# A hybrid decoder layer on one core: another way to the first half of x^T, squares moved to VectorE, a set of sums made a step later, the first gates' operands made earlier, and another last row

## The chip, the core and the metric

The kernel runs on one core of a Trainium2 chip. A core has TensorE (PE; its weight loads are listed as PEld), VectorE (DVE), ScalarE (ACT), GpSimd (POOL) and SyncE (SP), which here only issues DMAs. Each engine works through its own instructions strictly in the order in which they stand, and waits at an instruction until what it needs has been made. The metric is the time of one execution in microseconds (us), smaller is better. Times within a profile are counted from the first instruction.

## The reference

All is float32: 2048 positions of width 1024, one input projection to 6144 columns, two mixers, one output projection.

```python
xn = rms_norm(h, ln_g)
proj = jnp.einsum('bsd,de->bse', xn, w_in)
b_gate, c_gate, x_conv, g_conv, x_lru, g_lru = jnp.split(proj, splits, axis=-1)
y_conv = short_conv_mixer(b_gate, c_gate, x_conv, conv_w)
y_conv = headwise_rms_norm(y_conv, N_CONV_HEADS, conv_out_g) * jax.nn.silu(g_conv)
y_lru = rg_lru_mixer(x_lru, lru_conv_w, lru_conv_b, w_a, b_a, w_i, b_i, lam)
y_lru = headwise_rms_norm(y_lru, N_LRU_HEADS, lru_out_g) * jax.nn.silu(g_lru)
h = h + jnp.einsum('bse,ed->bsd', jnp.concatenate([y_conv, y_lru], axis=-1), w_out)
return rms_norm(h, final_g)
```

`rms_norm` divides each row of x by the root of its mean square. In `rg_lru_mixer` a width-4 convolution u goes through two block-diagonal maps (the gates), a is exp(8 r log_sigmoid(lam)), and a recurrence runs over the positions.

## The kernel before

**Products.** A float32 value is split into a high part (a cast by ScalarE to a type that TensorE multiplies at full rate) and a low part (value minus high part, a subtraction on VectorE or GpSimd, function `low`). A product is three matmuls: high by high, high by low, low by high (`mm`, L959). A 2x2 block product is done in the seven-product way: sums of blocks of the weights (tiles `s`) and of x^T (tiles `th`, `tl`, named T[0..6]; T[6] is the sixth sum, kept as `t6` until it is split). A group of matmuls is 4 pieces j of the contraction times 3.

**Steps.** A step is one set of output columns: `l` (the recurrence's input and gate path), `a` and `b` (the convolution mixer), `o` (output projection). The first three steps are plain: eight blocks each without sums. Step 0 works with c11, c21 on positions 0 to 511 and c12, c22 on positions 512 to 1023; steps 1 and 2 run 8 groups each in `plain`, and while they run the sums of x^T blocks are made (`bit`, functions done two per group by `after1`, then `after2`). From step 3 on a step has seven products, with an A bank whose content is copied out (`q1`, `u2`, `rr`) before the next product adds to it.

**The start.** Rows 0 to 511 of x (`x0[0..3]`) are loaded, squared on ScalarE (`norm_rows`), scaled by 1/root on VectorE, and turned into x^T by 128x128 transposes on TensorE (`turn`: four per 128x512 piece, 16 pieces for 1024 rows); a copy out of PSUM applies ln_g. Rows 512 to 1023 follow in the same way (`second`). The constant klam for the recurrence is made by small VectorE instructions at the very start (`make_klam`, L118 to L138).

**What sets the order.** The whole order is written by hand: the code is run once, and each engine gets its instructions as the code names them. `at(n, f)` puts f off by n calls of `tick()`; there is one tick per group of matmuls. So the recurrence of step 0 (`lru`, called with late=3) has its convolution c0, cj at ticks 1 to 3, `sth` (a cast of u on ScalarE) at 5+3, `stl` (two subtractions 64x1024 on VectorE, tiles `st`) at 6+3, the first gates at 8+3, their sigmoids at 9+3, the second gates at 10+3 (gates have two PSUM buffers, freed by the sigmoids), then products, Tanh, Exp, Sqrt, the scan `s5` and `finish`. `finish` scales a tile `gl` or `gb` (L633) and stores it by DMA to `yd`; these tiles have two buffers, so the step after next fills the buffer (put 22 and 21) only when that store has landed.

**The last row.** In the last step `put` combines each bank, adds the residual `xr`, squares on ScalarE, takes the root, scales by final_g on VectorE and stores; the two blocks of 128 positions go one after the other.

Of the kernel before, what the change touches and what calls it, by code (L numbers as in the profile page):

```python
# [38 lines left out]
def hymba_kernel(ctx: ExitStack, tc: tile.TileContext, x, xt, w_in, par, lamc, w_gate, w_out, final_g, out):  # L39
# [75 lines left out]
    def make_klam():  # L115
# [6 lines left out]
        nc.vector.tensor_scalar(out=acc, in0=s, scalar1=2.0, scalar2=None, op0=ALU.add)
# [390 lines left out]
    def norm_rows(b):
        junk = sp.tile([P, D], F32, tag="s", name="junk")
        ss = small.tile([P, 1], F32, tag="ss", bufs=4, name="ss")
        rs = small.tile([P, 1], F32, tag="rs", bufs=4, name="rs")
        nc.scalar.activation(out=junk, in_=x0[b], func=AF.Square, accum_out=ss)
        nc.scalar.activation(out=rs, in_=ss, func=AF.Sqrt, scale=1.0 / D, bias=eps)

        def scale():  # L520
            nc.vector.reciprocal(out=rs, in_=rs)
            nc.vector.tensor_scalar(out=x0[b], in0=x0[b], scalar1=rs, scalar2=0.0,
                                    op0=ALU.mult, op1=ALU.add)

        return scale

    def turn(c, kt, dst, act):
        pool, tag = ((pss, "s"), (psu, "u"))[act]
        tp = pool.tile([P, C], F32, tag=tag, name="tp")
        for b in range(NB):  # L530
            nc.tensor.transpose(tp[:, b * P:(b + 1) * P], x0[c * NB + b][:, kt * P:(kt + 1) * P], ident)
        g = pt[:, LN_G + kt:LN_G + kt + 1]
        if act:
            nc.scalar.activation(out=dst, in_=tp, func=AF.Copy, scale=g)
        else:
            nc.vector.tensor_scalar(out=dst, in0=tp, scalar1=g, scalar2=None, op0=ALU.mult)
# [793 lines left out]
```

## Time and profile before

| what | us |
|---|---|
| time, median of 3 runs (lowest to highest) | 1340.99 (1340.28 to 1343.42) |
| the profiled execution | 1336.38 |
| its span, first to last instruction | 1334.6 |
| TensorE busy, share of the span | 1293.2, 97% |
| VectorE busy | 1033.8, 77% |
| ScalarE busy | 747.1, 56% |
| GpSimd busy | 230.9, 17% |
| mean granted TensorE clock | 0.993 |

A busy TensorE is not one at its peak: matmuls overlap, so what counts is the distance between their starts and the places where it stands still. A row of the timeline is: start, duration, engine, line, operation, tiles out<-in, shape, count; in brackets the idle time just before and what ended it. A row of the view by windows gives the window, its length, then busy time and count of each engine, the granted clock, the share of the DMA engines and GB/s.

### The profile page before, as it was taken

The numbers are of one execution on the slowest core, as the hardware profiler recorded it, in microseconds if no ns is written. First come the engines' busy times: TensorE is split into PE (matmuls) and PEld (weight loads), VectorE is DVE, ScalarE is ACT, GpSimd is POOL, SyncE is SP. The second block draws the span as 40 slices with busy tenths as digits, with TensorE's granted clock in tenths as the row PEclk, the third lists the DMA queues.
The fourth block names the chain that finished last, engine by engine and source line by source line (L and its number), as shares of the span: only waits on it lengthen the run. The fifth ranks groups of instructions, "written<-read, shape, count | busy, mean of one in ns | idle before, by whom it ended". The sixth has DMA issues, their size and how long they took to land.

```text
span 1334.6 us, 16554 instructions
## 1 busy us (share of the span) xinstructions
PE 1293.2 (97%) x5648; PEld 1056.4 (79%) x5648; DVE 1033.8 (77%) x1245; ACT 747.1 (56%) x1139; POOL 230.9 (17%) x160
## 2 busy tenths in 40 slices
PE   6989999999999999899999999999999999999997
PEld 5867778787878787778888888888888888887886
DVE  7778888899989897978566675667549867648986
ACT  7476757575665757465544545354457433444543
POOL 2204343343344350202010101102010000000000
PEclk9989999999999999999999999999999999999999
DMA  7137897988889889453689999999779888797754
GB/s 290 32 111 254 288 255 281 286 317 295 327 282 336 291 284 327 149 162 111 215 308 304 335 347 332 349 340 365 244 269 324 260 224 238 278 384 258 250 178 165
DMA packets 158804, 355.27 MB, mean 266 GB/s; under 512 B 17920, under 2 KB 52736, under 8 KB 158720
## 3 DMA queue, kind: packets, MB, share of 16 engines
q1 hardware_dynamic: 158432, 353.90, 78.4%
q8 instruction: 45, 0.74, 0.2%
q14 instruction: 39, 0.32, 0.1%
q10 hardware_dynamic: 288, 0.32, 0.1%
HBM read 217.11 MB, written 137.04 MB: 265 GB/s over the span
## 4 chain that ended last, share of the span: by engine, by line
PE 50%; DVE 17%; DMA 12%; issue 8%; ACT 4%; SPq 1%; POOL 1%; DVEq 0%; ACTq 0%; POOLq 0%
PE bank L959 49%; DVE s L163 4%; DVE tl L163 2%; DMA raw<-in_w_in_dram 2%; DMA sd<-s 2%; DMA xr<-od 2%; PE gate L718 2%; DVE u L692 1%; DVE st L163 1%; DMA s<-so 1%; DVE raw L163 1%; DMA tl<-td 1%; DVE sums L623 1%; DVE gl L633 1%; ACT i L725 1%
## 5 line engine op out<-in xcount | busy, mean ns | idle before, releaser
L959 PE MATMUL bank<-th,s 128*128 128x512 f32 x3632 | 1134.2, 391 | 11.4 <-ACT q L1264 4.4
L959 PEld LDWEIGHTS bank<-th,s 128*128 128x128 f32 x3632 | 684.3, 188 | 161.9 <-ACT q L1264 5.7
L959 PE MATMUL bank<-tl,s 128*128 128x512 f32 x1816 | 709.5, 391 | 1.1 <-DVE tl L163 0.9
L959 PEld LDWEIGHTS bank<-tl,s 128*128 128x128 f32 x1816 | 341.9, 188 | 73.8 <-DVE tl L163 2.5
L163 POOL TENSOR_TENSOR s<-raw,s 128x512 fp32r<-128x512 f32 x62 | 111.4, 1809 | 254.1 <-ACT s L200 213.0
L200 ACT CAST s<-raw 128x512 fp32r<-128x512 f32 x140 | 85.0, 617 | 85.2 <-PE bank L959 39.2
L163 POOL TENSOR_TENSOR gb<-gb,sg 128x1024 f32<-128x1024 f32 x16 | 43.4, 2712 | 329.8 <-ACT sg L651 292.1
L163 DVE TENSOR_TENSOR s<-raw,s 128x512 fp32r<-128x512 f32 (+1 forms) x125 | 89.8, 741 | 8.3 <-ACT s L1017 4.4
L163 DVE TENSOR_TENSOR s<-s,s 128x512 fp32r<-128x512 f32 x105 | 85.6, 815 | 3.7 <-ACT s L200 3.7
L163 DVE TENSOR_TENSOR tl<-traw,th 128x512 fp32r<-128x512 f32 x85 | 62.8, 771 | 27.3 <-ACT th L438 13.4
L200 ACT CAST s<-s 128x512 fp32r<-128x512 f32 x105 | 64.6, 615 | 17.0 <-DVE s L163 15.9
L692 DVE SCALAR_TENSOR_TENSOR u<-xl,pt,u 128x1024 f32<-128x1024 f32 x48 | 64.4, 1341 | 6.3 <-ACT u L688 5.8
L1264 ACT COPY q<-bank 128x512 f32<-128x512 f32 x58 | 33.9, 584 | 54.5 <-PE bank L959 45.0
L802 DVE SCALAR_TENSOR_TENSOR t<-p,pt,t 128x1024 f32<-128x1024 f32 x32 | 46.5, 1454 | 14.7 <-ACT t L799 13.9
L725 ACT ACTIVATE r<-gate,pt 64x512 f32<-64x512 f32 x64 | 43.7, 683 | 18.7 <-PE gate L718 17.9
L163 DVE TENSOR_TENSOR st<-u,st 64x1024 fp32r<-64x1024 f32 x32 | 49.5, 1547 | 1.0
L1267 ACT COPY rr<-bank 128x512 f32<-128x512 f32 x31 | 18.1, 583 | 50.4 <-PE bank L959 50.4
L163 POOL TENSOR_TENSOR gl<-gl,sg 128x1024 f32<-128x1024 f32 x16 | 40.3, 2521 | 23.7 <-ACT sg L651 23.7
L725 ACT ACTIVATE i<-gate,pt 64x512 f32<-64x512 f32 x64 | 43.8, 684 | 1.1
L1267 ACT COPY u<-bank 128x512 f32<-128x512 f32 x27 | 15.8, 584 | 50.8 <-PE bank L959 50.7
L163 DVE TENSOR_TENSOR traw<-traw 128x512 f32<-128x512 f32 x60 | 41.8, 699 | 2.6 <-DMA traw<-in_w_out_dram 1.3
L163 DVE TENSOR_TENSOR raw<-raw,zr 128x512 f32<-128x512 f32 x64 | 41.1, 682 | 3.1 <-issue 1.8
(158 smaller groups left out, 1230.9 us busy)
## 6 DMA issues: line engine op xcount, KB each, us to landing
sd<-s SPq DMA_DIRECT2D x151, 512.0 KB
s<-sd SPq DMA_DIRECT2D x151, 512.0 KB
raw<-in_w_in_dram SPq DMA_DIRECT2D x104, 256.0 KB
raw<-yd SPq DMA_DIRECT2D x64, 256.0 KB
traw<-in_w_out_dram SPq DMA_DIRECT2D x64, 256.0 KB
so<-so SPq DMA_DIRECT2D x22, 512.0 KB
s<-so SPq DMA_DIRECT2D x22, 512.0 KB
yd<-gl SPq DMA_DIRECT2D x32, 256.0 KB
```

The lines of the kernel that those rows point to most:

```text
L163: (eng or nc.vector).tensor_tensor(out=out, in0=a, in1=b, op=op)
L200: nc.scalar.copy(dst[i][0], val(i))
L623: nc.vector.tensor_reduce(out=sums[0][:, kt * R:(kt + 1) * R].rearrange("p (q b) -> p q b", q=4), in_=y.rearrange("p (b q a) -> p q b a", ...
L633: nc.vector.scalar_tensor_tensor(out=sil, in0=y, scalar=gain, in1=sil, op0=ALU.mult, op1=ALU.mult)
L692: nc.vector.scalar_tensor_tensor(out=v["u"], in0=o1[:, 1 + j:1 + j + N2], scalar=lw[j], in1=v["u"], op0=ALU.mult, op1=ALU.add)
L718: nc.tensor.matmul(ps[j], v["gw"][n][:, j, :], v["st"][j][:, sl], start=(n == 0), stop=(n == 1))
L725: nc.scalar.activation(out=g_[hi, sl], in_=v["ps"][j][src], func=AF.Sigmoid, bias=pt[src, bias + k:bias + k + 1])
L802: nc.vector.scalar_tensor_tensor(out=tcur["t"], in0=p[:, 2 + j:2 + j + N2], scalar=cw[j], in1=tcur["t"], op0=ALU.mult, op1=ALU.add)
L959: nc.tensor.matmul(bank, a[:, js], b, start=start and n == 0, stop=stop and n == 2, skip_group_check=more)
L1264: nc.scalar.copy(q1, bk["A"])
L1267: nc.scalar.copy(u2, bk["A"])
```

## The change

It has these parts:

1. **x^T of the first half is loaded.** Positions 0 to 511 of x^T come from the transposed copy of x by DMA, two pieces (j and j+4) to a load, 128 x 2 x 512; so do pieces 0 to 3 of positions 512 to 1023. The rows of x are still loaded, for the squares. The roots of the four row blocks (`rs0`) are spread over the partitions by four transposes of a broadcast column into one PSUM bank (`spread`), and each piece is scaled in place by ln_g and that bank (`scaled_t`, one VectorE instruction). Pieces 4 to 7 of positions 512 to 1023 are still turned on TensorE (`turn`, 16 transposes), from rows of which only the right half is scaled.
2. **Two squares on VectorE**: rows 1 and 3 of the first half, by a multiply with a running sum; rows 0 and 2 stay on ScalarE, and one root serves all four. Rows 4, 5 and (6, 7) are squared and scaled one loop pass later than before.
3. **Fifty transposes** of the identity stand first on TensorE (`spin`).
4. **The rest of klam** (22 small VectorE instructions) is made after step 0.
5. **Sums.** `bit` casts first and subtracts one place later; t6 goes to other tiles; the split of the sixth sums moves from step 2 to step 3 (`sixth`).
6. **First gates.** `sth` and `stl` of step 0 come 3 ticks earlier (early=3).
7. **The last row** has a `put_last` of its own, in halves of 512 columns.

```diff
+    def square(b):
+        ss = ss0[b // NB][:, b % NB:b % NB + 1]
+        if b in (1, 3):
+            nc.vector.scalar_tensor_tensor(out=x0[b], in0=x0[b], scalar=1.0, in1=x0[b],
+                                           op0=ALU.mult, op1=ALU.mult, accum_out=ss)
+        else:
+            out = x0[b] if b < NB else sp.tile([P, D], F32, tag="s", name="junk")
+            nc.scalar.activation(out=out, in_=x0[b], func=AF.Square, accum_out=ss)
...
+    def spread(c):
+        rsb[c] = pss.tile([P, C], F32, tag="s", name="rsb")
         for b in range(NB):
+            nc.tensor.transpose(rsb[c][:, b * P:(b + 1) * P],
+                                rs0[c][:, b:b + 1].broadcast_to((P, P)), ident)
+
+    def scaled_t(c, kt, dst):
+        nc.vector.scalar_tensor_tensor(out=dst, in0=dst, scalar=pt[:, LN_G + kt:LN_G + kt + 1], in1=rsb[c],
+                                       op0=ALU.mult, op1=ALU.mult)
...
-                for slots, *fs in ((5, sth), (6, stl), (8, lambda: gates(0)), (9 - h, lambda: sigs(0)),
+                for slots, *fs in ((5 - early, sth), (6 - early, stl), (8, lambda: gates(0)), (9 - h, lambda: sigs(0)),
...
+        def put_last(which, bank, other):
+            i, d = which // 10 - 1, which % 10 - 1
+            tt(ob[i][:, half[d]], bank, other if which == 22 else xr[i][:, half[d]], ALU.add)
+            if which == 22:
+                tt(ob[1][:, half[1]], ob[1][:, half[1]], xr[1][:, half[1]], ALU.add)
+                square(1, 1, 0)
+                tt(xr[1][:, half[0]], xr[1][:, half[0]], sm_u2[0], ALU.add)
+                tt(xr[0][:, half[0]], xr[0][:, half[0]], sm_q1[0], ALU.add)
+            elif which == 11:
+                square(0, 0, 0)
+                bias(1)
+                tt(ob[1][:, half[1]], ob[1][:, half[1]], fg[0][:, half[1]], ALU.mult)
+            elif which == 12:
+                square(0, 1, 2)
+                bias(0)
+                root(0)
+                scaled(0, 0)
+            else:
+                square(1, 0, 2)
+                scaled(0, 1)
+                root(1)
+                scaled(1, 0)
+                nc.scalar.activation(out=ob[1][:, half[1]], in_=ob[1][:, half[1]], func=AF.Copy,
+                                     scale=sq[1][:, 3:4])
+                store(1, 1, nc.scalar)
...
+        spin(50)
+        klam_ = make_klam()
...
+        get_w[0]()
+        get_xt(0)
+        for f in get_w[1:]:
+            f()
+        get_row(4)
+        get_xt(1)
+        get_row(5)
+        get_xt(2)
+        get_row(6)
+        get_xt(3)
+        get_row(7)
...
+            if j:
+                rows(*((4,), (5,), (6, 7))[j - 1])
...
-                put = lru(0, 0, 3)
+                put = lru(0, 0, 3, 3)
...
+        klam_()
         second_half()
...
+        sixths = {1: (2, 1), 3: (0,), 4: (3,)}
...
+                if n == PLAIN:
+                    sixth(*sixths.get(s, ()))
```

Three places show how the order moves. The first is VectorE in steps 1 and 2 before: the last sums of x^T (`traw`, `t6`), a low part of step 2's weights (`s`), the product of the convolution mixer (`p`), the two subtractions `st` for the first gates, then the mixer's convolution (`t`).

```order
L163 TENSOR_TENSOR traw_543<-traw_543,traw_273 128x512
L163 TENSOR_TENSOR tl_787<-traw_543,th_786 128x512
L163 TENSOR_TENSOR t6_790<-traw_273,traw_543 128x512
L163 TENSOR_TENSOR s_792<-raw_598,s_792 128x512
L163 TENSOR_TENSOR p_617<-p_617,xx_807 128x512
L163 TENSOR_TENSOR st_781<-u_619,st_781 64x1024
L163 TENSOR_TENSOR st_782<-u_619,st_782 64x1024
L802 SCALAR_TENSOR_TENSOR t_822<-p_617,pt_164,t_822 128x1024 x2
```

The same engine with the change, from the place where the `st` pair now stands.

```order
L166 TENSOR_TENSOR s_670<-raw_558,s_670 128x512
L166 TENSOR_TENSOR traw_257<-traw_263,traw_257 128x512
L166 TENSOR_TENSOR traw_263<-traw_264,traw_263 128x512
L166 TENSOR_TENSOR st_696<-u_600,st_696 64x1024
L166 TENSOR_TENSOR st_697<-u_600,st_697 64x1024
L166 TENSOR_TENSOR traw_264<-traw_264,traw_257 128x512
L166 TENSOR_TENSOR tl_704<-traw_257,th_703 128x512
L166 TENSOR_TENSOR traw_257<-traw_257,traw_264 128x512
```

The `st` pair is now 14 instructions of 128x512 ahead of the convolution `t`, where it was right ahead of it; the product `p` that `t` needs comes last.

The second is VectorE around the scan of step 0's recurrence (in step 3), before: `u` is the drive, `r` the scan's tile, `s1`, `s2` and `s` belong to step 4's weights, the last row is the scaling of `gl` whose store frees a buffer.

```order
L743 SCALAR_TENSOR_TENSOR u_619<-r_857,u_619 128x1024
L163 TENSOR_TENSOR u_619<-T_957,u_619 128x1024
L163 TENSOR_TENSOR s1_1049<-raw_1012,raw_1014 128x512
L163 TENSOR_TENSOR s2_1051<-s1_1049,raw_1011 128x512
L752 SCALAR_TENSOR_TENSOR r_857<-r_857,u_619 128x1024
L755 COPY hl_187<-r_857 128x1
L163 TENSOR_TENSOR s_1055<-raw_813,s_1055 128x512
L163 TENSOR_TENSOR s_1025<-s2_841,s_1025 128x512
L163 TENSOR_TENSOR raw_1012<-raw_1011,raw_1012 128x512
L633 SCALAR_TENSOR_TENSOR gl_568<-r_857,pt_164,gl_568 128x1024
```

With the change:

```order
L759 SCALAR_TENSOR_TENSOR u_600<-r_836,u_600 128x1024
L166 TENSOR_TENSOR u_600<-T_928,u_600 128x1024
L166 TENSOR_TENSOR tl_1013<-traw_257,th_1012 128x512
L166 TENSOR_TENSOR tl_1017<-rr_677,th_1016 128x512
L166 TENSOR_TENSOR s1_1020<-raw_975,raw_977 128x512
L166 TENSOR_TENSOR s2_1022<-s1_1020,raw_974 128x512
L768 SCALAR_TENSOR_TENSOR r_836<-r_836,u_600 128x1024
L771 COPY hl_187<-r_836 128x1
L166 TENSOR_TENSOR s_1026<-raw_794,s_1026 128x512
L166 TENSOR_TENSOR s_988<-s2_820,s_988 128x512
L166 TENSOR_TENSOR raw_975<-raw_974,raw_975 128x512
L649 SCALAR_TENSOR_TENSOR gl_527<-r_836,pt_164,gl_527 128x1024
```

Two low parts of sixth sums (`tl`) now stand ahead of the scan; their casts (`th`) stand on ScalarE behind the table load and the sigmoid of `gb`.

The third is VectorE at the end of the program, before, from the product of block 0's first half (`ob` is the output tile, `xr` the residual, `fg` final_g).

```order
L163 TENSOR_TENSOR ob_11054<-bank_11157,q1_11076 128x512
L163 TENSOR_TENSOR ob_11054<-ob_11054,xr_11078 128x1024
L163 TENSOR_TENSOR ob_11055<-bank_11121,xr_11057 128x512
L902 RECIPROCAL rs_11186<-rs_11186 128x1
L903 SCALAR_TENSOR_TENSOR ob_11054<-ob_11054,rs_11186,fg_9905 128x1024
L163 TENSOR_TENSOR rs_11204<-ss_11203 128x1
L511 RECIPROCAL rs_11204<-rs_11204 128x1
L920 SCALAR_TENSOR_TENSOR ob_11055<-ob_11055,rs_11204,fg_9905 128x512 x2
```

With the change:

```order
L166 TENSOR_TENSOR ob_11033<-bank_11044,xr_11059 128x512
L946 TENSOR_SCALAR sq_11035<-sq_11035 128x1
L952 RECIPROCAL sq_11035<-sq_11035 128x1
L959 SCALAR_TENSOR_TENSOR ob_11033<-ob_11033,sq_11035,fg_9884 128x512
L166 TENSOR_TENSOR ob_11034<-bank_11102,xr_11038 128x512
L959 SCALAR_TENSOR_TENSOR ob_11033<-ob_11033,sq_11035,fg_9884 128x512
L952 RECIPROCAL sq_11036<-sq_11036 128x1
L959 SCALAR_TENSOR_TENSOR ob_11034<-ob_11034,sq_11036,fg_9884 128x512
```

Behind the last bank (`bank_11102`) there are now two scalings of 128x512 on VectorE, where there were one of 128x1024 and two of 128x512; the other half is scaled on ScalarE.

More of the change, by code (lines that the diff above doesn't have):

```diff
@@ L527, in turn @@
-    def turn(c, kt, dst, act):
-        pool, tag = ((pss, "s"), (psu, "u"))[act]
-        tp = pool.tile([P, C], F32, tag=tag, name="tp")
-        for b in range(NB):
[L531 to L536, printed above, removed]
+    rs0 = [small.tile([P, NB], F32, tag="rs4", bufs=2, name="rs0") for _ in range(2)]
@@ new lines, in hymba_kernel, with spin, turn @@
+    spun = [None]
+    def spin(n):
+        if spun[0] is None:
+            spun[0] = psn.tile([P, 2 * KT * R], F32, tag="sums", name="spin")
+        for _ in range(n):
+            nc.tensor.transpose(spun[0][:, 0:P], ident, ident)
+    def turn(kt, dst):
+        tp = psu.tile([P, C], F32, tag="u", name="tp")
+        for b in range(NB):
+            nc.tensor.transpose(tp[:, b * P:(b + 1) * P], x0[NB + b][:, kt * P:(kt + 1) * P], ident)
+        nc.scalar.activation(out=dst, in_=tp, func=AF.Copy, scale=pt[:, LN_G + kt:LN_G + kt + 1])
@@ L949, in put, with square, bias @@
                 fin(1)
-        return put
+        half = [slice(d * C, (d + 1) * C) for d in range(2)]
+        sq = [small.tile([P, 4], F32, tag="sq", bufs=2, name="sq") for _ in range(2)] if last else None
+        def square(i, d, n):
+            nc.scalar.activation(out=xr[i][:, half[d]], in_=ob[i][:, half[d]], func=AF.Square,
+                                 accum_out=sq[i][:, n:n + 1])
+        def bias(i):
+            nc.vector.tensor_scalar(out=sq[i][:, 1:2], in0=sq[i][:, 0:1], scalar1=1.0 / D, scalar2=EPS,
+                                    op0=ALU.mult, op1=ALU.add)
@@ new lines, in root, with store, scaled @@
+        def root(i):
+            rs = sq[i][:, 3:4]
+            nc.scalar.activation(out=rs, in_=sq[i][:, 2:3], func=AF.Sqrt, scale=1.0 / D, bias=sq[i][:, 1:2])
+            nc.vector.reciprocal(out=rs, in_=rs)
+        def store(i, d, eng):
+            tb = 2 * m + i
+            eng.dma_start(out[tb * P:(tb + 1) * P, half[d]], ob[i][:, half[d]])
+        def scaled(i, d):
+            nc.vector.scalar_tensor_tensor(out=ob[i][:, half[d]], in0=ob[i][:, half[d]], scalar=sq[i][:, 3:4],
+                                           in1=fg[0][:, half[d]], op0=ALU.mult, op1=ALU.mult)
+            store(i, d, nc.sync)
@@ L1170, in after2, with sixth @@
                 low(tr[j][1], T[3, j])
+        def sixth(*js):
+            for j in js:
                 T[6, j] = t_tile(6, j)
```

156 lines of the change are left out of this document (67 added, 89 removed).

## The prediction

> **What bounds the kernel.** I read the page, then TensorE's waits, the windows round the places found, and the timeline there. The first two rows below are of the page and of TensorE's waits, the rest windows.
>
> ```profile
> PE 1293.2 (97%) x5648; PEld 1056.4 (79%) x5648; DVE 1033.8 (77%) x1245; ACT 747.1 (56%) x1139; POOL 230.9 (17%) x160
> ...
> PE gate L718 <- ACT hp L807: 5.5, 1, 5.5
> ...
> PE gate L718 <- DVE st L163: 4.1, 7, 1.3
> ...
> 44.70:72.00 27.30, 27.30 (x121) 22.31 (x119) 23.10 (x30) 13.48 (x22) 4.31 (x4) 1.00 0.05 18
> 72.00:77.50 5.50, 0.03 (x1) 0.00 (x0) 4.07 (x7) 3.85 (x7) 0.00 (x0) 0.69 0.00 0
> 77.50:101.80 24.30, 22.94 (x92) 18.09 (x92) 19.08 (x25) 20.37 (x30) 0.10 (x1) 0.93 0.50 174
> ...
> 600.00:1000.00 400.00, 400.00 (x1762) 330.40 (x1761) 259.17 (x290) 206.36 (x279) 44.85 (x28) 1.00 0.85 293
> ```
>
> TensorE is the bound nearly throughout: from 600 to 1000 it starts a matmul every 400/1762 = 0.227 us, so a group of 12 takes 2.72. The largest single hole is 72 to 77.5, where the first gates wait and the clock drops (0.69; behind it 0.93 over 24.3 us, worth 1.7). Seven waits of gates for `st` say that VectorE is late in later steps too. The timeline of the hole and of the end of the program:
>
> ```profile
> 75.47 0.68 DVE L163 TENSOR_TENSOR p<-p,xx 128x512 f32<-128x512 f32 x1
> 76.19 2.47 DVE L163 TENSOR_TENSOR st<-u,st 64x1024 fp32r<-64x1024 f32 x2
> 76.25 1.15 ACT L799 ACTIVATE t<-p,pt 128x1024 f32<-128x1024 f32 x1 [1.62 <-DVE p L163]
> ...
> 77.55 0.77 PE L718 MATMUL gate<-st,bh 128*128 128x512 f32 x1 [5.53 <-ACT hp L807]
> ...
> 80.88 0.68 ACT L725 ACTIVATE i<-gate,pt 64x512 f32<-64x512 f32 x1
> ...
> 86.75 0.40 PE L959 MATMUL bank<-th,s 128*128 128x512 f32 x1
> ...
> 1326.49 0.39 PE L959 MATMUL bank<-th,s 128*128 128x512 f32 x1
> ...
> 1327.78 1.29 DVE L903 SCALAR_TENSOR_TENSOR ob<-ob,rs,fg 128x1024 f32<-128x1024 f32 x1
> ...
> 1331.15 0.35 ACTq L922 DMA_DIRECT2D out_dram<-ob  x1
> ```
>
> TensorE stood for the `st` pair, which VectorE began only at 76.19; behind the last matmul the last store is issued 4.4 us later.
>
> **Step 0: nothing.** The rows of its terms, in order of time:
>
> ```profile
> 1.21 0.29 POOL masks.py:199 TENSOR_SCALAR_AFFINE_SELECT ident<-ident 128x128 f32<-128x128 f32 x1
> 5.14 1.06 ACT L517 ACTIVATE junk<-x 128x1024 f32<-128x1024 f32 x1 [0.45 <-DMA x<-in_x_dram]
> ...
> 4.00:6.00 2.00, 0.00 (x0) 0.00 (x0) 1.66 (x11) 1.54 (x3) 0.00 (x0) 1.00 1.04 420
> ...
> 11.76 3.04 PE L531 MATMUL tp<-ident,x 128*128 128x128 f32 x13 [0.89 <-DVE x L522]
> 14.45 0.78 PE L959 MATMUL bank<-th,s 128*128 128x512 f32 x1
> 18.42 1.03 PE L531 MATMUL tp<-ident,x 128*128 128x128 f32 x8
> ...
> 30.18 0.61 ACT L1068 CAST th<-traw 128x512 fp32r<-128x512 f32 x1
> 31.43 0.75 DVE L536 TENSOR_SCALAR traw<-tp,pt 128x512 f32<-128x512 f32 x1
> ...
> 33.43 1.30 POOL L163 TENSOR_TENSOR tl<-traw,th 128x512 fp32r<-128x512 f32 x1 [0.76 <-ACT th L248]
> 33.90 1.37 DVE L163 TENSOR_TENSOR s<-raw,s 128x512 fp32r<-128x512 f32 x1 [0.35 <-ACT s L1017]
> ...
> 44.86 0.59 ACT L781 COPY gl<-bank 128x512 f32<-128x512 f32 x1 [2.15 <-PE bank L959]
> ```
>
> The first row block lands at 5.1; at 420 GB/s 0.52 MB takes 1.25, so the fourth lands at 8.9, the first x^T load at 10.8, the next three at 15.2, 17.7, 20.2 and the last row block at 21.5. The fourth square, now on VectorE, ends near 10.2 (1.3, as L903 of the same shape; 0.75 to 1.5 are the ends), root, reciprocal and four transposes give the spread roots at 11.6, scaling (0.75, as L536) and cast bring the first matmul to 13.0 against 14.45. Forty transposes fewer (64 before; 16 and 8 now) are 40 x 0.13 = 5.2 us less on TensorE. But TensorE is not what is late here. Per piece j the chain is two scalings, two casts, a subtraction on VectorE, one of 1.3 on GpSimd; and a VectorE subtraction that meets GpSimd's waits (33.90: 1.37 where it takes 0.69 alone). Going through this engine by engine, the groups of j = 0 to 3 end at 17.9, 21.9, 24.6 and 28.1. ScalarE's order then has the squares of rows 6 and 7 at 26.2 and 27.4 (1.06 and their sums), root at 28.6, scaling of row 7 until 29.95, transposes, copy 0.7, two casts, GpSimd until 33.8, so the first half-group of c12 and c22 ends at 33.8 + 8 x 0.227 = 35.7, and three more with two sets of four transposes at 35.7 + 8.2 + 1.0 = 44.9. Before, `gl` is copied when c22 ends, 44.86. I take no change; ends: 1.5 earlier (the two waits for GpSimd don't happen) and 1.9 later (the third rival). The x^T loads' speed isn't shown at this place; at half speed the last row would land at 26.5, still ahead of its square, so the price is nothing until then.
>
> **Steps 1 and 2: a lead of 2.** Rows:
>
> ```profile
> 3.21 0.17 DVE L122 TENSOR_SCALAR kl<-kl 128x8 f32<-128x8 f32 x1 [0.27 <-ACT kl L120]
> ...
> 7.26 0.16 DVE L138 TENSOR_SCALAR klam<-kl 128x8 f32<-128x8 f32 x1
> ...
> DVE tl L163 <- ACT th L1104: 3.6, 5, 1.4
> ...
> 46.49 0.69 DVE L163 TENSOR_TENSOR s<-raw,s 128x512 fp32r<-128x512 f32 x1 [3.34 <-ACT s L1017]
> ...
> ACT r L725 <- PE gate L718: 1.3, 2, 1.0
> ...
> ACT gb L781 <- PE bank L959: 0.8, 1, 0.8
> ...
> 101.24 0.58 ACT L1264 COPY q<-bank 128x512 f32<-128x512 f32 x1
> ```
>
> The `st` pair goes ahead of 14 instructions and ends near 69.7, so the gates start when TensorE gets there, at 72: 5.5 us and the slow clock behind them are gone. But VectorE's list gets longer: the rest of klam, 7.42 - 3.21 = 4.2 us, now stands behind `s` at 46.5, where nothing hides it, and the 3.6 us of waits for casts go (cast and subtraction stand further apart, VectorE is later). From 46.49 to the end of `st` at 78.66 VectorE took 32.2; now 46.6 + 32.2 + 4.2 - 3.6, less 0.7 for one wait for GpSimd that is shorter, gives `p`, now last, at 78.7 against 76.15. So ScalarE's `t` starts 2.5 later. The sigmoids stand behind it: they end at 80.88 + 0.68 + 2.5 less 0.3 of wait = 83.8, and the second gates need the buffers that these free. TensorE stands there instead, about 80 to 83.8, and the next group starts near 84.2, not 86.75. ScalarE from `t` to the copy `q`: 25.0 before; the waits for TensorE (1.3 + 0.8) and four casts of sixth sums (4 x 0.6) go: 78.75 + 25.0 - 2.1 - 2.4 = 99.3 against 101.24. Lead: 1.9.
>
> **Step 3: most of it given back.** Rows:
>
> ```profile
> 101.83 1.28 ACT L651 ACT_TABLE_LOAD   x1
> ...
> 103.33 2.28 DVE L752 TENSOR_TENSOR_SCAN r<-r,u 128x1024 f32<-128x1024 f32 x1
> ...
> 106.66 2.84 POOL L163 TENSOR_TENSOR gb<-gb,sg 128x1024 f32<-128x1024 f32 x1
> 107.18 2.88 DVE L163 TENSOR_TENSOR s<-s,s 128x512 fp32r<-128x512 f32 x1
> ...
> 110.58 1.27 DVE L633 SCALAR_TENSOR_TENSOR gl<-r,pt,gl 128x1024 f32<-128x1024 f32 x1
> ...
> 115.37 0.69 DVE L163 TENSOR_TENSOR gl<-bank,u 128x512 f32<-128x512 f32 x1 [2.91 <-DMA yd<-gl]
> ```
>
> Two sixth subtractions now stand ahead of the scan, and their casts behind `q`, the table load and the sigmoid: 99.3 + 0.5 + 1.3 + 1.1 + 0.6 = 102.8. With both (1.3) and the two sums (1.3) the scan starts at 105.4, 2.1 later than before. Then `gb` on GpSimd (105.3 to 108.1) lies beside the scan and costs less than at 107.18, where one subtraction waited 2.2 for it; three subtractions, the first ending 0.6 behind GpSimd, and `gl` is scaled at 109.9 against 110.58. The store and the fill of the next `gl` follow at a fixed distance (115.37), and behind that fill stand `xl`, `u` and the copy `q` that TensorE needs in step 4. So **0.7 us** are left. From there on the order is the same, and VectorE is still what gates wait for, so a lead of TensorE alone is lost and 0.7 stays. Ends: -1.5 and the full 1.9 + 1.5.
>
> **The last row: 1.1 us.** The last bank is combined at 1327.4 (VectorE has just scaled a half), squared on ScalarE until 1328.85 with its sum, root 1329.16, reciprocal 1329.4, scaled until 1330.1 on VectorE and ScalarE side by side; last issue 1330.15 against 1331.15, and 256 KB less queued ahead of it. At L903's 1.29 a half is 0.7; the ScalarE half is as L781's copy, 0.6. Ends 0.7 and 1.5.
>
> **Sum.** 0 + 0.7 + 1.1 = 1.8. The profiled execution took 1336.38, so 1334.6; the runs' median is 4.6 above that execution, so I forecast 1340.99 - 1.8 = **1339.2**.
>
> **Rivals.** (1) *The lead is kept.* If ScalarE gets to the sigmoids earlier, or the scan isn't held, TensorE keeps 1.9 + 1.5 and up to the whole hole, 5.5 and 1.7 of slow clock: with the last row's 1.1 that is 4.5 to 8.3, **1332.7 to 1336.5**. For it: gates wait for `st` by 4.1 in all, so VectorE is near enough; against: klam's 4.2 have no cover. (2) *The st pair isn't what the gates lacked* (the change doesn't do what it says): the hole stays, 1340. Against: the pair's start at 76.19. (3) *The spin stays slow.* Ready at 1.5, 50 transposes take 50 x 0.13 = 6.4 at the pace of 18.42, 50 x 0.21 = 10.7 at that of 11.76 (12 intervals of 0.21): they end at 12.2, behind the roots, and all of step 0 is 1.9 later: **1341.1**. The Trainium skill, "TensorE: Matmul & The Clock Gate", section "Part 4: PE-mode transpose", says that transposes don't raise the clock; by that rule the spin would do this. Against it: by 18.42 transposes ran fast, 6.7 us after the slow ones began, and nearly half of that time was transposes. I give it 0.08. (4) *Slower:* the new order still makes VectorE wait 3.6 for casts in steps 1 and 2 (two `st` casts now stand ahead of them on ScalarE). Then `p` is at 82.3, all of step 3 is 3.6 later, from the point where those waits exceed 0.7: 1339.2 + 3.6 = **1342.8**; together with (3) 1344.7.
>
> **Chances.** A measurement tells about 0.3% from no change, 4 us. Forecast 0.48, (1) 0.34, (2) 0.02, (3) 0.08, (4) 0.08. Of these (1) is faster by over 4 us but for a tenth, which the forecast's upper end makes up; (3) and (4) are slower than before, by over 4 only together or with more delay in step 0, about a third of their 0.16: faster 0.34, same 0.61, slower 0.05. The range takes in most of (1), and (4): 1333.0 to 1343.0.
>
> **What would show it.** Right: gates of step 0 start near 72, TensorE stands before the second gates near 80 to 84, the scan later than 103.3, `gl` scaled near 110. Wrong: a matmul stream without a hole from 72 to 100, step 0's c22 copied well before 44 or after 46, or `gl<-bank` before 113.

## The result and the profile after

The changed kernel takes 1348.51 us (median of 6 runs, 1346.93 to 1350.18), the kernel before 1342.55 on the same chip (6 runs, 1340.28 to 1343.42): ratio 1.0051, interval 1.0040 to 1.0062. It is **slower by 6 us**; the forecast was 1.8 faster. On another chip (first experiment) it is 3.9 slower. The profiled execution took 1350.07, span 1347.9. That is 13.7 more than the profiled execution of before, over twice what the medians differ by: the latter (1336.38) is 3.9 below the fastest of the six runs of before. So the two traces are compared here place by place and not by their ends.

The windows of the changed kernel at the same times as those of before, in the last row the third of them before, and some of TensorE's waits (us in all, how often, the longest):

```profile
72.00:77.50 5.50, 5.50 (x24) 4.24 (x23) 5.44 (x9) 1.59 (x3) 0.00 (x0) 1.00 0.00 0
77.50:101.80 24.30, 21.34 (x80) 15.94 (x79) 19.00 (x27) 19.13 (x29) 0.10 (x1) 0.86 0.40 133
101.80:126.00 24.20, 18.64 (x74) 14.60 (x73) 17.07 (x18) 14.80 (x23) 5.54 (x3) 0.93 0.52 193
...
101.80:126.00 24.20, 23.89 (x104) 19.45 (x105) 21.19 (x21) 14.24 (x23) 9.40 (x5) 1.00 0.72 256
```

```profile
PE bank L997 <- ACT q L1340: 6.5, 3, 2.9
PE bank L997 <- ACT u L1346: 5.0, 2, 4.2
...
PE bank L997 <- ACT th L251: 3.3, 1, 3.3
...
PE bank L997 <- DVE s L166: 2.0, 1, 2.0
```

The hole at 72 is gone, as forecast: 24 matmuls in 5.5 us where there was one. But the next two windows start 80 and 74 matmuls instead of 92 and 104. A wait of 3.3 for `th` (the start), one of 4.2 for the copy `u` (step 3) and one of 2.0 for `s` (step 2) are new; the waits for the copies `q` were 4.4 in all before.

The timeline of the start, by engine:

```profile
10.66 0.18 DVE L526 RECIPROCAL rs<-rs 128x4 f32<-128x4 f32 x1 [0.43 <-ACT rs L525]
10.89 0.65 PE L533 MATMUL rsb<-ident,rs 128*128 128x128 f32 x4 [2.11 <-DVE rs L526]
...
12.96 1.41 DVE L537 SCALAR_TENSOR_TENSOR traw<-traw,pt,rsb 128x512 f32<-128x512 f32 x2 [2.12 <-DMA raw<-in_w_in_dram]
...
14.86 0.79 PE L997 MATMUL bank<-th,s 128*128 128x512 f32 x1 [3.32 <-ACT th L251]
...
48.17 0.59 ACT L797 COPY gl<-bank 128x512 f32<-128x512 f32 x1 [2.09 <-PE bank L997]
```

The roots are ready at 10.8 and spread at 11.5, a little ahead of the forecast's 11.6. VectorE waits from 10.8, 2.1 us, until the first x^T load is there too, scales at 12.96 instead of 11.6, and c22 is copied at 48.17 instead of 44.9. (The row names the piece of `w_in` that is in flight with that load; in other executions the same wait is put down to `in_xt_dram`, below.)

The timeline of steps 1 to 3:

```profile
69.21 4.33 DVE L166 TENSOR_TENSOR st<-u,st 64x1024 fp32r<-64x1024 f32 x2 [0.27 <-ACT st L719]
...
81.66 0.69 DVE L166 TENSOR_TENSOR p<-p,xx 128x512 f32<-128x512 f32 x1
...
86.67 0.68 ACT L741 ACTIVATE i<-gate,pt 64x512 f32<-64x512 f32 x1
...
103.70 0.58 ACT L1340 COPY q<-bank 128x512 f32<-128x512 f32 x1
...
104.30 1.28 ACT L667 ACT_TABLE_LOAD   x1
...
105.59 1.06 ACT L667 ACTIVATE sg<-gb 128x1024 f32<-128x1024 f32 x1
...
106.56 0.60 ACT L1244 CAST th<-traw 128x512 fp32r<-128x512 f32 x1
...
107.19 0.69 DVE L166 TENSOR_TENSOR tl<-traw,th 128x512 fp32r<-128x512 f32 x1 [2.64 <-ACT th L1244]
...
109.13 1.67 DVE L166 TENSOR_TENSOR s<-s,raw 128x512 f32<-128x512 f32 x1
...
110.21 2.85 POOL L166 TENSOR_TENSOR gb<-gb,sg 128x1024 f32<-128x1024 f32 x1
...
110.72 4.49 DVE L768 TENSOR_TENSOR_SCAN r<-r,u 128x1024 f32<-128x1024 f32 x1
...
117.14 1.28 DVE L649 SCALAR_TENSOR_TENSOR gl<-r,pt,gl 128x1024 f32<-128x1024 f32 x1
...
118.33 0.69 DVE L166 TENSOR_TENSOR tl<-u,th 128x512 fp32r<-128x512 f32 x1
...
119.11 0.59 ACT L1346 COPY u<-bank 128x512 f32<-128x512 f32 x1 [1.19 <-DVE tl L166]
...
119.75 0.50 PE L997 MATMUL bank<-th,s 128*128 128x512 f32 x1 [4.24 <-ACT u L1346]
...
123.12 0.69 DVE L166 TENSOR_TENSOR gl<-bank,u 128x512 f32<-128x512 f32 x1 [2.89 <-DMA yd<-gl]
```

Read from the copy `q` on: before, the scan started 2.1 behind `q` (103.33 - 101.24) and took 2.28; now it starts 7.0 behind and takes 4.49. VectorE waits 2.64 for the cast of a sixth, which stands on ScalarE behind the table load and the sigmoid `sg`. So the scan comes to lie beside GpSimd's `gb`, where before a subtraction lay (107.18, 2.88 us). Then ScalarE's copy into `u` waits until VectorE, past the scan and `gl`, has read the old `u` for a sixth sum (118.33), and TensorE waits for that copy. `gl<-bank` is 7.75 later than before (115.37).

The end of the program:

```profile
1340.44 0.39 PE L997 MATMUL bank<-th,s 128*128 128x512 f32 x1
...
1343.94 0.38 ACTq L956 DMA_DIRECT2D out_dram<-ob  x1
```

From the last matmul to the last store's issue it is 3.50 instead of 4.66.

### The profile page after: what moved, and what is told of

It is laid out like the page before. It is cut to its first block, busy times and chain, and to the rows that moved or that the text cites. A ratio compares the mean times of both kernels' runs of the same rounds, so it can differ in the third digit from the quotient of the medians.

```text
span 1347.9 us, 16573 instructions
## 1 busy us (share of the span) xinstructions
PE 1304.1 (97%) x5658; PEld 1062.4 (79%) x5658; DVE 1036.4 (77%) x1248; ACT 743.0 (55%) x1129; POOL 229.1 (17%) x160
## 4 chain that ended last, share of the span: by engine, by line
PE 45%; DMA 4%; DVE 3%; issue 1%; ACT 0%; SPq 0%; DVEq 0%
PE bank L997 44%; DMA xr<-od 2%; DMA s<-so 1%; PE gate L734 1%; DVE s L166 1%; DMA tl<-td 1%; DVE raw L166 1%; DVE ob L166 0%; DMA yd<-gl 0%; DMA traw<-in_w_out_dram 0%; DVE tl L166 0%; DMA yd<-gb 0%; DVE ob L919 0%; DVE st L166 0%; DVE sums L639 0%
## 5 line engine op out<-in xcount | busy, mean ns | idle before, releaser
L166 DVE TENSOR_TENSOR s<-s,s 128x512 fp32r<-128x512 f32 x105 | 82.1, 782 | 6.7 <-ACT s L203 6.7
L818 DVE SCALAR_TENSOR_TENSOR t<-p,pt,t 128x1024 f32<-128x1024 f32 x32 | 46.6, 1455 | 16.0 <-ACT t L815 15.2
L166 DVE TENSOR_TENSOR traw<-traw 128x512 f32<-128x512 f32 x62 | 45.8, 741 | 3.1 <-DMA traw<-in_w_out_dram 1.8
L166 DVE TENSOR_TENSOR raw<-raw 128x512 f32<-128x512 f32 x41 | 44.6, 1087 | 0.2
```

Of the source, the lines that this page charges most:

```text
L166: (eng or nc.vector).tensor_tensor(out=out, in0=a, in1=b, op=op)
L818: nc.vector.scalar_tensor_tensor(out=tcur["t"], in0=p[:, 2 + j:2 + j + N2], scalar=cw[j], in1=tcur["t"], op0=ALU.mult, op1=ALU.add)
```

## Experiments

Medians of before differ by 1 us from chip to chip, so kernels are compared by their ratio to the runs of before taken beside them; it comes from all runs and can differ from the quotient of the two medians by up to 0.0007, 0.9 us. The columns `q`, scan and c22 are read from the trace of one execution of each kernel, as above. Names with a_ are the changed kernel with something taken back or added, those with b_ and c_ are the kernel before with some parts of the change, those with s_ are `a_klam_sixths_back` with something added.

| run | median us | before beside it | ratio (interval) | c22 | q | scan: behind q, long |
|---|---|---|---|---|---|---|
| after_again | 1344.20 | 1340.26 | 1.0027 (1.0017 to 1.0037) | 46.59 | 100.85 | 7.0, 4.50 |
| a_sixths_back | 1340.43 | 1340.13 | 1.0003 (0.9994 to 1.0011) | 46.57 | 102.61 | 2.1, 2.29 |
| a_klam_start | 1338.68 | 1340.13 | 0.9991 (0.9980 to 1.0002) | 48.27 | 98.43 | 7.0, 4.49 |
| a_old_start | 1343.15 | 1340.13 | 1.0021 (1.0012 to 1.0030) | 44.57 | 100.05 | 7.0, 4.49 |
| b_gates_last | 1335.32 | 1340.13 | 0.9962 (0.9951 to 0.9974) | 44.93 | 96.84 | 2.1, 2.28 |
| c_sixths_behind | 1333.52 | 1340.26 | 0.9945 (0.9932 to 0.9957) | 45.14 | 95.29 | 2.1, 2.28 |
| b_sixths_moved | 1338.08 | 1339.63 | 0.9988 (0.9980 to 0.9997) | 45.13 | 95.29 | 7.0, 4.49 |
| b_gates_last_2 | 1334.32 | 1339.63 | 0.9963 (0.9951 to 0.9976) | 44.77 | 96.67 | 2.1, 2.28 |
| c_sixths_behind_2 | 1333.93 | 1339.63 | 0.9951 (0.9938 to 0.9965) | 45.30 | 95.47 | 2.1, 2.28 |
| a_klam_sixths_back | 1336.72 | 1339.63 | 0.9978 (0.9968 to 0.9987) | 46.75 | 98.66 | 2.1, 2.28 |
| a_load_w_first | 1344.18 | 1340.26 | 1.0028 (1.0017 to 1.0039) | 48.82 | 104.22 | 7.0, 4.50 |
| a_no_spin | 1342.94 | 1340.26 | 1.0019 (1.0010 to 1.0028) | 46.44 | 102.31 | 7.0, 4.50 |
| s_bridge | 1335.90 | 1340.01 | 0.9969 (0.9958 to 0.9980) | 47.37 | 99.28 | 2.1, 2.29 |
| s_touch | 1336.78 | 1340.01 | 0.9972 (0.9961 to 0.9983) | 47.71 | 99.62 | 2.1, 2.28 |
| b_last | 1339.05 | 1340.01 | 0.9995 (0.9986 to 1.0003) | 45.18 | 103.07 | 2.1, 2.28 |

### The change once more, and its parts taken back one by one

`after_again` has no edit.

> The changed kernel once more, so that it is timed beside the same runs of the kernel before as the parts are. Theory A (three losses: start 3.3, sixths ahead of the scan 4.1 with a hole of 4.6 on TensorE, less a lead of about 2 and the last row's 1.1): c22's copy at 48.2, q at 103.7, scan 7.0 behind it and 4.5 long, as in its first profile, and 5 to 8 us slower than before. The further 6.4 us that its first profile lost between the gates of 144 and 275 (waits of 1.7 and 2.4 us, each with a slow clock behind it) belong to single executions; without them the gates of step 9 stand near 329, not 335. Theory B (these 6.4 us belong to the program): gates near 335 again.

3.9 slower than before, less than the 5 to 8 expected; c22 is at 46.59 and `q` at 100.85, not at 48.2 and 103.7 as in the first profile. The gates of step 9 stand at 327.5, near the 329 of theory A. Both executions have the hole of step 3, and both have a wait near 205 and one near 255; only the first lost the clock behind the latter two. Its windows of the wait at 207 and of what follows:

```profile
207.00:209.30 2.30, 0.77 (x3) 0.38 (x3) 2.27 (x2) 0.40 (x1) 1.01 (x1) 1.00 1.03 421
209.30:213.00 3.70, 3.70 (x10) 2.87 (x11) 3.67 (x7) 0.62 (x1) 0.00 (x0) 0.54 1.03 420
```

and those of `after_again` at the same place of the program:

```profile
203.00:206.00 3.00, 1.35 (x6) 0.66 (x5) 2.94 (x3) 0.59 (x1) 1.40 (x1) 1.00 1.03 421
206.00:210.00 4.00, 4.00 (x19) 3.30 (x18) 3.90 (x7) 1.50 (x3) 0.00 (x0) 1.00 1.03 419
```

Granted clock (third from the end) 0.54 there, 1.00 here, 10 matmuls in 3.7 us there, 19 in 4.0 here. TensorE's wait of 1.51 us for `st` is followed by the slow clock in one execution (there a wait of 0.29 stands just ahead of it) and not in the next. The 10 matmuls instead of some 18 are worth about 1.6 us, an estimate from these two rows, and there are two such places; from `q` to the gates of step 9 the first execution falls behind by another 4.7.

`a_sixths_back` puts the sixth sums back into step 2:

```diff
+                T[6, j] = t_tile(6, j)
+                nc.scalar.copy(T[6, j][0], t6[j])
+                low(t6[j], T[6, j])
...
-                if n == PLAIN:
-                    sixth(*sixths.get(s, ()))
```

> The changed kernel with the sixth sums put back: their casts and subtractions in step 2 (four last slots), as before the change, and their own buffers (q1, u2, rr, t6). Theory A (the move of the sixths is what turned the change into a loss: two subtractions stand ahead of the scan and their casts behind the table load and sigmoid, so the scan of step 0 starts 7.0 us behind the copy q instead of 2.1, beside GpSimd's 2.8 us subtraction, and the copy into u waits for the sixth's subtraction out of u): the scan starts 2 to 3.5 us behind q and takes 2.3, TensorE's hole of 4.6 us at 115 goes, gl<-bank comes near 119 instead of 123.1, and the time falls by 3.5 to 5.5 us against the changed kernel (about 1343 to 1345 on the scale of the medians 1342.5 and 1348.5). Theory B (the start alone, 3.3 us later, and VectorE's klam are the loss; the sixths cost the same wherever they stand): another hole of the same size opens in step 2 or 3 and the time stays within 1.5 us of the changed kernel.

Theory A. The scan is 2.1 behind `q` and 2.3 long again, the hole of 4.6 is gone, `gl<-bank` is at 116.76, and the ratio falls from 1.0027 (`after_again`) to 1.0003: 3.2 us, a little under the 3.5 to 5.5 expected.

`a_klam_start` puts klam's 22 operations back to the start:

```diff
-        klam_ = make_klam()
+        make_klam()()
...
-        klam_()
         second_half()
```

> The changed kernel with the 22 small klam operations (4.1 us on VectorE) back at the start, where VectorE waits for the first row blocks from 2.9 to 6.4 us. Theory A (klam's 4.1 us lie bare on VectorE in steps 1 and 2): the first square starts 0.7 later at most, c22's copy stays at 48.2 within 0.7, the st pair and p come 3 to 4 us earlier (p ends near 78.5 instead of 82.3), TensorE's waits before and at the second gates (2.1 and 1.2 us at 79.4 and 84.6) shrink by 2 to 3 us. What reaches the end depends on the scan: if the sixths in front of the scan eat it, the gain at the end is 0 to 1.5 us; if VectorE alone set step 3, it is 3 to 4. Theory B (the lead in step 2 is set by TensorE and ScalarE, klam is hidden): less than 0.5 us at q and at the end.

Theory A, and more reaches the end than expected: `q` at 98.43 although c22 is as late as in the first profile, ratio 0.9991 against 1.0027, 4.8 us. With the sixths in step 2 the same edit is worth 3.4 (`a_sixths_back` 1.0003, `a_klam_sixths_back` 0.9978). Against the first profile the last `p` is 4.0 earlier and `q` 5.3; TensorE's wait of 2.0 for `s` is gone too.

`a_old_start` takes the start of before and leaves the rest (edit: the code from the first load to the first `second(0)`, and the helpers it calls, as before the change).

> The changed kernel with the start of before (x rows normalised, 64 transposes, squares on ScalarE, no warm-up transposes, old order of loads), everything behind it as changed, klam's operations where the change puts them. Theory A (the new start is 3.3 us slower: first x^T load lands at 12.9 with 2 KB packets at half speed, and the clock falls twice in gaps of TensorE): c22's copy at 44.9 instead of 48.2, and 2.5 to 4 us less at the end (about 1345). Theory B (step 3 sets the time whatever the start; the lead of a start is lost there): c22 at 44.9 but under 1 us at the end.

Theory B, as it stands: c22 is at 44.57, but only 0.8 us less at the end, within the intervals. Its trace shows the wait for `s` (1.95 us, until 78.2), two waits at the second gates and a slow clock from 80 to 86; `q` is 0.8 ahead of `after_again`'s. So with klam's operations on VectorE in step 1 most of the start's gain is lost on the way to `q`; a comparison without them follows.

`b_gates_last` is before with the early `st` pair (`lru(0, 0, 3, 3)`), the new order of the casts in `bit` and `after1`, and the last row.

> The kernel before with two parts of the change alone: the st pair three slots earlier, the last row's new order (and the casts of the eighths of x ordered as in the change). Old start, klam at the start, sixths in step 2. Theory A (these two parts are the gain, the others the loss): TensorE's hole of 5.5 us at 72 and the slow clock behind it go, p comes about 1 us earlier or later than 76.2, the second gates near 82, the tail from the last matmul to the last issue 3.5 instead of 4.7; 4 to 7 us faster than before (about 1336 to 1338.5). Theory B (the lead is given back at the scan in any case): 1 to 2 us faster, the last row alone.

Theory A: 4.8 us faster (4 to 7 were expected), and 5.3 in its second run.

### Where the sixths stand

`b_sixths_moved`, `b_gates_last_2` and `c_sixths_behind_2` ran together and differ in the sixths alone. The third has

```diff
-            t6[j] = aux("t6") if j == 3 else sm(("q1", "u2", "rr")[j])
+            t6[j] = sm("u2") if j == 0 else aux("t6") if j == 1 else tr[j][2]
...
+        sixths = {3: (0, 1), 4: (2, 3)}
```

and the first the change's own lines, `{1: (2, 1), 3: (0,), 4: (3,)}`.

> The kernel before with the st pair three slots earlier and the last row's new order (as the run that had just these), and the sixth sums' casts and subtractions put behind the scan and the scaled gl of step 0: places 3 and 4 of that step, sums 0 and 1 in buffers u2 and aux, sums 2 and 3 in place. Theory A (four casts of sixths on ScalarE delay the copy q by 2.1 us, for which TensorE waits 3.1 at 94; behind the scan both engines have idle time of 2.1 and 2.9 us): q near 94.7 instead of 96.8, the wait of 3.1 at 94 falls to about 1, the slow clock behind it goes; the scan stays 2.1 behind q and 2.3 long; 2 to 4 us faster than the run without this move, 1331.5 to 1333.5 where before is 1340.1. Theory B (any place of the sixths in step 3 costs what it saves): the copy into u waits again and the time is within 1 us of 1335.3 or above.

> Old start, klam at the start, early st pair, new last row, and the sixth sums moved as the change moves them (places 1, 3, 4 of step 0's lru step, sum 0 in u2): the change without its new start and without its late klam. It differs from the next two kernels of this call only in where the sixths stand: step 2 (b_gates_last_2), ahead of the scan (this one), behind the scan (c_sixths_behind_2). Theory A (the place in front of the scan costs): q near 95.3 as with the sixths behind, scan 7.0 behind q (102.3) and 4.5 long beside GpSimd's subtraction, a hole of 4.4 on TensorE before the copy into u; 3 to 4.5 us slower than c_sixths_behind_2 and 1.5 to 3 slower than b_gates_last_2. Theory B (with VectorE relieved of klam the sixths in front of the scan find idle time): the hole is under 2 us and the time within 1 us of b_gates_last_2.

> The run with old start, klam at the start, early st pair and new last row once more, sixths in step 2, for a comparison on one chip. Theory A and B alike: about 4.8 us faster than before (ratio 0.996); by theory A between the other two.

> The same with the sixths behind the scan once more. Theory A: scan 2.1 behind q, TensorE's wait before q's group 1.5, 1.5 to 2.5 us faster than b_gates_last_2 (ratio to before about 0.9945). Theory B (the gain of 1.8 seen so far is the spread of single sessions): within 0.7 us of b_gates_last_2.

TensorE's waits from 90 to 125 in `b_sixths_moved`, then VectorE's timeline there:

```profile
PE bank L984 <- ACT u L1297: 4.2, 1, 4.2
PE bank L984 <- ACT q L1291: 1.3, 1, 1.3
```

```profile
98.78 0.69 DVE L166 TENSOR_TENSOR tl<-traw,th 128x512 fp32r<-128x512 f32 x1 [2.65 <-ACT th L1195]
...
102.31 4.49 DVE L755 TENSOR_TENSOR_SCAN r<-r,u 128x1024 f32<-128x1024 f32 x1
...
109.92 0.68 DVE L166 TENSOR_TENSOR tl<-u,th 128x512 fp32r<-128x512 f32 x1
```

The same two views of `c_sixths_behind_2`:

```profile
PE bank L984 <- ACT q L1291: 1.3, 1, 1.3
PE bank L984 <- ACT u L1297: 0.2, 1, 0.2
```

```profile
97.55 2.28 DVE L755 TENSOR_TENSOR_SCAN r<-r,u 128x1024 f32<-128x1024 f32 x1
...
99.95 1.52 DVE L166 TENSOR_TENSOR s<-raw,s 128x512 fp32r<-128x512 f32 x1
101.40 2.90 DVE L166 TENSOR_TENSOR s<-s,s 128x512 fp32r<-128x512 f32 x1
...
104.81 1.27 DVE L636 SCALAR_TENSOR_TENSOR gl<-r,pt,gl 128x1024 f32<-128x1024 f32 x1
...
106.01 0.68 DVE L166 TENSOR_TENSOR tl<-u,th 128x512 fp32r<-128x512 f32 x1
```

With the sixths ahead of the scan 1338.08, in step 2 1334.32, behind the scan 1333.93. So the place in front of the scan costs 3.8 against step 2 (3.4 by the ratios; 1.5 to 3 were expected) and 4.2 against the place behind it: theory A of `b_sixths_moved`. That the place behind the scan beats step 2 isn't settled: where both ran together it is 0.4 us by the medians, as theory B of `c_sixths_behind_2` has it, and 1.6 by the ratios, as theory A has it, with overlapping intervals of five runs each; the runs on two other chips gave 1.8 and 2.3. In step 2 the four casts hold up `q`, for which TensorE waits 3.1 instead of 1.3. The kernel with the sixths behind the scan beats before and the changed kernel: in its two runs it is 6.7 and 5.7 us faster than before.

The long scan is not what costs the 4 us. Behind the scan, too, VectorE pays for what GpSimd does beside it: the two subtractions at 99.95 and 101.40 take 3.0 us more than their 0.69 each, while in `b_sixths_moved` the second of the two sums (1.67) and the scan (4.49) take 3.2 more. What differs is in front of the scan: VectorE's wait of 2.65 for the cast and the two subtractions of sixths, 1.2. These 3.9 are nearly all of the 4.1 by which the subtraction that reads `u` stands further behind `q` (14.6 and 10.5). ScalarE's copy into `u` waits for that subtraction in both kernels; TensorE then waits 4.2 for the copy in the one and 0.2 in the other.

### The start

`a_klam_sixths_back` is the change with klam at the start and the sixths in step 2, so that it differs from `b_gates_last_2` in the start alone.

> The changed kernel with klam at the start and the sixths in step 2: it differs from b_gates_last_2 only in the start (x^T loaded and scaled in place, warm-up transposes, squares of two row blocks on VectorE). Theory A (the new start is slower and nothing behind it makes up for it): c22 at 46.6, or 48.2 where the clock falls near 35, against 44.9; 1.5 to 3.3 us slower than b_gates_last_2. Theory B (the start's delay is lost in the waits behind it, as the run with the old start seemed to say, which gained 0.8): within 1 us of b_gates_last_2.

Theory A: 1336.72 against 1334.32, 2.4 us (2.0 by the ratios), with c22 at 46.75 against 44.77.

`a_load_w_first` issues the first x^T load behind all four pieces of `w_in`:

```diff
-        get_w[0]()
-        get_xt(0)
-        for f in get_w[1:]:
+        for f in get_w:
             f()
+        get_xt(0)
```

> The changed kernel with the first x^T load issued behind all four first pieces of w_in instead of behind one. Theory A (the packets of 2 KB took up to 174 ns instead of 84 from 8.5 to 12 us because x^T and w_in were fetched together): packets at 84 ns, the pieces of w_in in by 11, x^T near 12.1, first matmul near 13.8 instead of 14.9, c22 0.5 to 1 us earlier. Theory B (the first x^T load is slow by itself): the pieces of w_in in by 11, x^T near 13.5, first matmul near 15, c22 as before or later. In either case no more than 1 us at the end.

Theory B. The pieces of `w_in` now come at full rate, and the slow stretch moves with the x^T load. The windows of the change, then those of this run (the last number is GB/s):

```profile
8.00:9.00 1.00, 0.79 (x8) 0.55 (x5) 0.00 (x1) 0.86 (x2) 0.00 (x0) 1.00 1.06 385
9.00:10.00 1.00, 0.00 (x0) 0.00 (x0) 1.00 (x1) 0.35 (x1) 0.00 (x0) 1.00 1.01 223
10.00:11.00 1.00, 0.10 (x1) 0.11 (x2) 0.41 (x3) 0.57 (x2) 0.65 (x1) 1.00 0.93 209
```

```profile
9.00:10.00 1.00, 0.00 (x0) 0.00 (x0) 0.90 (x1) 0.22 (x1) 0.00 (x0) 1.00 1.06 408
...
11.00:12.00 1.00, 0.65 (x4) 0.41 (x4) 0.00 (x0) 0.24 (x1) 0.74 (x1) 1.00 0.90 279
12.00:13.00 1.00, 0.00 (x0) 0.00 (x0) 0.00 (x0) 0.00 (x0) 0.00 (x0) 0.52 1.00 295
```

In the packet records 2 KB take 84 to 92 ns in the mean of each half microsecond from 8 to 11 and up to 197 from 11 to 14. Many of these packets still take 84 and some take up to 446: in 12 to 13, 32 of 54 take over 120. VectorE begins to scale at 14.05, and nothing is gained.

`a_no_spin` leaves out the 50 transposes (`-        spin(50)`), which the outputs don't depend on.

> The changed kernel without its 50 warm-up transposes. Theory A (the clock they raise is lost again in the gaps of 2.4 and 3.6 us behind them, at 11.8, before the first matmul; the start is set by VectorE and ScalarE, not by TensorE): first matmul at 14.9 within 0.2, matmuls 0.43 apart until about 21.5 as with them, c22 within 0.7 us of 48.2, the time within 1.5 us of the changed kernel. Theory B (they shorten the slow stretch): the slow clock lasts until 24 or later, c22 1 to 3 us later.

Theory A: first matmul 14.66, c22 46.44 (46.59 in `after_again`), and the time is no longer than with them.

`s_bridge` adds `spin(34)` behind `spread(0)` to `a_klam_sixths_back`; `s_touch` adds to it an early read of 64 bytes of each row of x^T:

```diff
+    touch = aux("touch")[:, 0:KT * 16].rearrange("p (k t) -> p k t", k=KT)
+    nc.scalar.dma_start(touch, xt.rearrange("(k p) t -> p k t", p=P)[:, :, 0:16])
```

> New start, klam at the start, sixths in step 2 (as the run that differed from the old start by 2.4 us), and 34 more warm-up transposes between the four that spread the roots and the first matmul, which fill TensorE's gap of 3.6 us there. Theory A (the start is late because of x^T: VectorE waits for its first load until 13.0, and behind that VectorE, ScalarE and GpSimd set the pace): the first matmuls are 0.23 apart instead of 0.43, but c22 stays within 0.5 us of 46.6 and the time within 1 us of 1336.7 (ratio to before 0.9978). Theory B (the slow clock from 15 to 21 makes the start late): c22 1 to 2 us earlier and as much at the end.

> The same start without the further transposes, and a small early read of x^T: 64 bytes of each of its 1024 rows, fetched by ScalarE's queue at 1 us into a spare buffer. Theory A (the first 2.5 us of loads from x^T go at half the packet rate because that tensor is read for the first time): the packets of the first x^T load take 84 ns, it lands near 11.6 instead of 13.0, first matmul near 13.5, c22 1 us or more earlier than 46.6. Theory B (the half rate belongs to that load's own place in the stream, or to its shape): packets up to 170 ns again, first matmul at 14.8.

In `s_bridge` the clock fell as the added transposes began (granted 0.50 from 12 to 14), so that they held TensorE until 17.1 and the first matmul came later, not earlier; from there matmuls are 0.23 apart where they don't wait. The first x^T load, c22 and the window behind them:

```profile
13.73 1.41 DVE L537 SCALAR_TENSOR_TENSOR traw<-traw,pt,rsb 128x512 f32<-128x512 f32 x2 [2.47 <-DMA traw<-in_xt_dram]
...
47.37 0.59 ACT L797 COPY gl<-bank 128x512 f32<-128x512 f32 x1 [2.09 <-PE bank L997]
...
33.00:41.00 8.00, 6.80 (x30) 5.06 (x31) 5.17 (x7) 5.79 (x11) 3.47 (x3) 1.00 0.54 195
```

c22 is copied 33.6 behind the start of that scaling. So it is in `after_again`, `a_sixths_back`, `a_klam_sixths_back`, `a_no_spin` and `s_touch` (33.5 to 33.8), with first matmuls anywhere from 14.7 to 17.1 and fast or slow from there to 21. **The x^T load sets the start, not the clock there:** theory A of `s_bridge`, though c22 is 0.8 from 46.6 and not within 0.5, as the scaling began 0.6 later. The evidence is this fixed distance; no run got the load in earlier. Another slow stretch does cost: in the first profile, `a_klam_start` and `a_load_w_first` the granted clock from 33 to 41 is 0.79, and c22 comes 34.8 to 35.2 behind, 1.0 to 1.7 more. `s_touch` had its load at half rate again (209 GB/s from 10 to 11), theory B, though the first matmul is at 15.9 and not at 14.8: that the tensor is read for the first time is not the cause, as far as 64 bytes of each row can tell.

### The last row alone

`b_last` is before with `put_last` and nothing else.

> The kernel before with the last row's new order alone. The prediction's term was 1.1 us. Theory A: from the last matmul to the last store's issue 3.5 us instead of 4.7, the rest as before, 0.7 to 1.5 us faster (ratio 0.9990 to 0.9995), so that of the 5.2 us that it gained together with the early st pair, some 4 belong to the pair. Theory B (the two belong together, or the last row is worth more): 2 us or more, or none.

The last issue comes 3.50 behind the last matmul (1333.71 and 1330.21), as expected. It is 0.96 us faster by the medians; the interval includes no change.

## Why the prediction was wrong

**Right: the last row.** 1.1 was forecast; it is 1.16 in the trace and 0.96 in `b_last`, whose interval includes no change.

**Right: steps 1 and 2.** The hole at 72 closed. `p` ended at 82.35, forecast 78.7 and the start 3.3 later; the sigmoids at 87.35, forecast 83.8 and the same 3.3. Klam's 4.2 without cover were measured as 3.4 and 4.8. The lead of 1.9 at `q` is there too: `after_again` has c22 1.73 later than before and `q` 0.39 earlier, a lead of 2.1. In the first profile it is 0.9: the slow clock behind the hole at 79.4 lasted longer there (granted 0.50 from 84 to 90, in `after_again` from 82 to 84). TensorE stood a little ahead of the place forecast, 2.0 us for `s` until 81.8 and then 0.8 at the second gates.

**Wrong: step 0, "nothing", measured 2.4 at the end.** The step that failed is the price of the x^T loads' speed: "at half speed the last row would land at 26.5, still ahead of its square, so the price is nothing until then". That weighed the end of the stream. The first load is waited for too: VectorE scaled at 12.96, 1.4 later than the 11.6 for which the forecast had reckoned, and c22 follows such a start by 33.6 where the clock holds near 35. From 11.6 that gives 45.2, so the rest of the step's chain was right. The clock near 35 adds 1.0 to 1.7 in some executions. Rival (3), which also had step 0 late, by 1.9, fell: the spin ended at 8.8, not 12.2, and without it c22 is the same.

The windows of `after_again` show the transposes getting faster, 12 and then 21 in 2 us:

```profile
4.00:6.00 2.00, 2.00 (x12) 2.00 (x11) 0.00 (x0) 1.61 (x3) 0.00 (x0) 1.00 1.04 416
6.00:8.00 2.00, 2.00 (x21) 2.00 (x19) 1.23 (x2) 0.60 (x3) 0.00 (x0) 1.00 0.99 405
```

The Trainium skill, "TensorE: Matmul & The Clock Gate", section "Part 4: PE-mode transpose", says that transposes don't raise the clock; here the pace of 50 of them in a row nearly doubled. That goes by the pace alone: the profile's granted clock reads 1.00 in both windows.

**Wrong: step 3, "most of it given back", 1.2 forecast, 5.4 measured.** From one copy `q` to the next it is 25.0 us in `after_again` (100.85 to 125.86) and 19.6 before (101.24 to 120.83). (The 3.8 of the comparison of the sixths is less, because without the sixths in step 2 `q` itself comes 1.4 earlier: 95.29 and 96.67.) The order was seen rightly: casts of sixths behind table load and sigmoid, subtractions ahead of the scan.

The step that failed is the price of GpSimd's work: "Then `gb` on GpSimd (105.3 to 108.1) lies beside the scan and costs less than at 107.18". At 107.18 a subtraction took 2.88 instead of 0.69, 2.2 more; the scan takes 4.49 instead of 2.28, in all six kernels with this order, 2.2 more again. The forecast had `gl` scaled 4.5 behind the start of the scan, and it is 6.4. Another 0.9 lies ahead of it: the scan was put 6.1 behind `q` (105.4 and 99.3) and is 7.0 behind it, as the second of the two sums takes 1.67 beside GpSimd. "The store and the fill of the next `gl` follow at a fixed distance" did not hold either: from the scaling of `gl` to the fill 4.8 before and 6.0 now; why is open.

The way by which the delay reaches TensorE was not seen either: the buffer of sixth sum 0 is `u2`, which ScalarE fills again in the same step, so TensorE stands 4.4 us (115.12 to 119.75, less a matmul's 0.23) for a subtraction behind the late scan.

**The sum by places.** In `after_again` step 0 is 1.7 later, the lead to `q` is 2.1, 5.4 are given back and the last row saves 1.2 (from the first profile): 3.9 slower, as by its median. The forecast had 0, 1.9, 1.2 and 1.1. (The ends of the two traces are 7.5 apart; the rest arises behind these places, where one execution differs from the next, and the one of before was a short one.)

**The sum by runs.** Early pair with the casts' order -4.2 (`b_gates_last_2` 5.3, less the last row's 1.1), last row -1.1, klam +3.4 to +4.8, sixths +3.8, start +2.4: 4.3 to 5.7 slower, measured 3.9 and 6.0. Rival (2) fell with the hole, and the lead of (1) ended at the scan. (4) had the time of `p` right, 82.3, by luck: VectorE's waits for casts from 47 to 83, on which it rests, went from 3.6 to 0.3 (those for the `st` pair), as the forecast had it, and `p` is late by the start.

Open is why the first x^T load runs at half rate.
